# Decoder trunk on one core: block sums queued behind the inverse root, the low half of each hidden pair one pair later, and another order in the last stage

## Chip, core and metric

The kernel runs on one core of one Trainium2 chip. The metric is the device time of one execution in microseconds (us); lower is better. The engines are named as in the profile: PE (matrix products and transposes), PEld (its weight load), DVE (vector), ACT (scalar, activations), POOL (GpSimd) and SP (which issues most DMAs). Each engine works through its own instructions in order and waits on semaphores for the others. A small "q" behind an engine's name is its instruction queue, which issues DMAs.

## What is computed

Two decoder layers over 512 tokens of width 1024, in float32. The change touches the squared-ReLU MLP, which ends both layers, and the final RMS norm:

```python
def squared_relu_mlp(h, w1, w2):
    return jnp.square(jax.nn.relu(h @ w1)) @ w2
...
        x = x + squared_relu_mlp(rms_norm(x, norm_mlp[layer]), mlp_w1[layer], mlp_w2[layer])
...
    return rms_norm(x, final_norm)
```

with a hidden width of 4096, and rms_norm(x, g) = x / sqrt(mean(x^2) + eps) * g. Between the two MLPs stand the shared key/value projection and the attention of the second layer, which the change leaves alone.

## The kernel before

**Number format.** Each float32 matrix is split into a hi and a lo part in float16, and each product is three matmuls: hi x hi, hi x lo, lo x hi (lines 341 to 343 in the up stages, 550 to 552 in the down stages). The hi is written by ACT, the lo (value less hi) by DVE.

**Stages.** An MLP is up, down, up, down, with half of the hidden width each time (`first_half`, then `mlp_down` again).

- **Up stage** (`mlp_up`, lines 487 to 506): eight pairs of hidden chunks. A pair takes 48 matmuls of 512 columns into two PSUM banks out of six (a, b, c twice each). Then DVE takes the relu and scales it by the tokens' inverse root of the norm (line 499, tile `ml_t`, one buffer), ACT squares it (line 501, tile `ml_z`), POOL forms four block sums of the square (line 503), ACT writes the hi part `rh` (line 504) and DVE the lo part `rl` (line 505). In the first up stage of a layer the inverse root is computed while the first pair is on PE: PE sums the squares (`ss.rstd`), ACT takes the square root and DVE does five small operations (`rstd_of`, lines 295 to 306); PE spreads the result over the partitions (line 312) and ACT scales it into the tile `rb` (line 317).
- **Down stage** (`mlp_down`, lines 536 to 574): four passes, one for each pair of output chunks. A pass runs over eight chunks c and computes seven block products instead of eight (the form with sums and differences of 2x2 blocks by Strassen and Winograd): 21 matmuls of 256 columns for each c. The seven results lie in four banks, a a b b in even passes and c c d e in odd ones. `combine` (lines 508 to 534) adds the seven results of a finished pass into the residual X: one copy on ACT (`dn_p`, line 520) and nine operations on DVE. It is a generator whose parts are drawn one by one (`next(post)`) behind the c loop of the following pass.
- **Last down stage** (layer 1, second half): besides, `mid_b` transposes the chunks of X that are finished to token-major form (`token_major`): after c = 5 of a pass PE transposes into a bank (tag a or c), ACT takes a square with a sum for the final norm (line 1162) and a copy (line 1177), and POOL multiplies the copy by the gains (line 1178). The copies must be done before the next pass writes the same banks. In the last pass the eight chunks are cut: c 0 to 3 for all seven products, then each product by itself over c 4 to 7 in a written order (`last_b`), so that `stt` additions, transposes, squares, the inverse root of two token tiles, the scaling and the stores to `out` (`store`, lines 1188 to 1203) follow each other.

**Weights.** `pieces` lists all weight pieces in order. `load_piece` issues the DMAs on SP's queue, `convert_piece` turns a piece into hi (ACT) and lo (DVE): 128x1024 pieces for an up stage (tiles `wst`, `whi`, `wlo`; lines 195 and 196), and for a down stage blocks of two chunks, for which DVE first forms the four block sums `W_SUMS` (line 182) in the loaded tile, then hi (line 184) and lo (line 185, 128x1792). Three loaded blocks and four converted ones fit; a loaded block's buffer is free for the next DMA when its lo is written, a converted one's when PE has used it. `ahead()` converts up to two pieces, or three blocks, ahead of use; `drain(ahead())` is where this stands in the program.

**What sets the order.** Lines are traced in program order, but a scheduling pass of the framework puts each engine's instructions in the order in which they are expected to become ready. So the block sums of a down stage stand far ahead of their place in the program, between the instructions of the up stage. `tc.issue_after(ins)` puts those instructions of its block that run on the engine of `ins` behind `ins` in that order, without a semaphore.

Of the kernel before, what the change touches and what calls it, by code (L numbers as in the profile page):

```python
# [2 lines left out]

# [1 line left out]

# [43 lines left out]
def body(ctx, tc, x, rel_bias, norm_mix, norm_mlp, mlp_w1, mlp_w2, a_w_in, a_conv_w, a_w_out,  # L49
# [121 lines left out]
    def convert_piece(step=1024):  # L171

        i = pos["cv"]
        if i >= len(pieces):
            return
        _, shape, sc = pieces[i]
        t = staged.pop(i)
        pos["cv"] += 1
        if shape is None:
            b = t.rearrange("p (k b n) -> p k b n", k=2, n=128)  # L180
            for e, o, x, y in W_SUMS:
                DVE.tensor_tensor(b[:, :, o], b[:, :, x], b[:, :, y], op=e)  # L182
            hi, lo = (wk[0].tile([128, 2, 7, 128], F16, name=n, bufs=NW2) for n in ("whi2", "wlo2"))
            ACT.activation(hi, b[:, :, 1:], AF.Copy, scale=sc)  # L184
            DVE.scalar_tensor_tensor(lo, b[:, :, 1:], sc, hi, op0=OP.mult, op1=OP.subtract)  # L185
            ready[i] = (hi, lo)
            yield
        else:
            a, n = shape
            hi = wpool.tile([128, PIECE], F16, name="whi", bufs=NW)  # L190
            lo = wpool.tile([128, PIECE], F16, name="wlo", bufs=NW)
            for s in range(0, a * n, step):
                e = min(s + step, a * n)
                w = t[:, s:e]
                ACT.activation(hi[:, s:e], w, AF.Copy, scale=sc)  # L195
                DVE.scalar_tensor_tensor(lo[:, s:e], w, sc, hi[:, s:e], op0=OP.mult, op1=OP.subtract)  # L196
# [90 lines left out]
    def split_gain(dst, c, src, gname):  # L287
# [3 lines left out]
        DVE.scalar_tensor_tensor(dst[1][:, c], src, g, dst[0][:, c], op0=OP.mult, op1=OP.subtract)  # L291
        return hi

    def rstd_of(ss):
# [10 lines left out]
        DVE.scalar_tensor_tensor(r, t, 1.5, r, op0=OP.add, op1=OP.mult)  # L305
        return r

    def broadcast_rows(r):
# [177 lines left out]

    def mlp_up(xs, ss, rh, half, rb):
        turn[0] = 1
        for p in range(8):
            ph = [acc(), acc()]  # L490
            first = p == 0 and half == 0
            pair(xs, ph, mid=ss.rstd if first else None)
            if first:
                pr = broadcast_rows(ss.r)
                rb = row_tile(pr, math.sqrt(SR) / (SW * SX))
            drain(ahead())
            t = wk[0].tile([128, 2, S], F32, name="ml_t", bufs=1)
            for m in range(2):
                DVE.scalar_tensor_tensor(t[:, m], ph[m], 0.0, rb, op0=OP.max, op1=OP.mult)  # L499
            z = wk[0].tile([128, 8, 256], F32, name="ml_z", bufs=2)  # L500
            ACT.activation(z[:, 0:4].rearrange("p (m k) n -> p m (k n)", m=2), t, AF.Square)  # L501
            for e, o, a, b in R_SUMS:
                POOL.tensor_tensor(z[:, o], z[:, a], z[:, b], op=e)  # L503
            ACT.activation(rh[0][:, p], z[:, 1:8], AF.Copy)  # L504
            DVE.tensor_tensor(rh[1][:, p], z[:, 1:8], rh[0][:, p], op=OP.subtract)  # L505
        return rb

    def combine(p, acc7, done):

        sc = 1.0 / (SR * SW2)  # L510
        P1, P2, P6, P7, P5, P3, P4 = acc7
        X1, X2 = X[:, 2 * p + 1], X[:, 2 * p]
        n1, n2 = slice(256, 512), slice(0, 256)
        both = X[:, 2 * p:2 * p + 2, n2]

        def stt(o, ps, y):
            DVE.scalar_tensor_tensor(o, ps, sc, y, op0=OP.mult, op1=OP.add)

        p1 = wk[0].tile([128, 256], F32, name="dn_p", bufs=1)
        ACT.activation(p1, P1, AF.Copy, scale=sc)  # L520
# [10 lines left out]
        E.tensor_tensor(both, both, wv, op=OP.add)  # L531
        stt(X2[:, n1], P4, X2[:, n1])
        E.tensor_tensor(X2[:, n1], X2[:, n1], wv[:, 0], op=OP.add)
        yield
        if done:
            yield from done(p)

    def mlp_down(rh, done, mid=None, last=None):

        post = iter(())  # L540
        for p in range(4):
# [13 lines left out]
            for c in range(0, 4 if late else 8, 2):  # L555
                w = next_piece()
                for k in range(2):
                    for i in range(7):
                        product(i, c + k, [u[:, k] for u in w])
                    if c + k == 5 and mid:  # L560
                        mid(p)
                    if k == 0:
                        drain(ahead())
                    next(post, None)
            if late:
                drain(post)
                if mid:
# [3 lines left out]
                return  # L571
            drain(post)
            post = combine(p, acc7, done)
        drain(post)

    def first_half(hp, xs, ss):
# [568 lines left out]
    with pool("hidden_b") as hp:  # L1145
# [12 lines left out]
            return fng[p // 2][:, (p % 2) * 256:(p % 2) * 256 + n * 128]  # L1158

        def square(v, t, k):  # L1160
            junk = hp.tile([128, 2, S], F32, name="ml_t", bufs=1)[:, 0, 0:v.shape[1]]
            ACT.activation(junk, v, AF.Square, accum_out=ssf[:, t, k:k + 1])

        def turn_tokens(ps, t, tiles):
# [3 lines left out]
        def token_major(p, h, tag):  # L1168
# [4 lines left out]
            for i in range(2):  # L1173
                t = 2 * h + i
                v, o = ps[:, i * 256:(i + 1) * 256], xt[t][:, p * 256:(p + 1) * 256]
                square(v, t, p)
                ACT.activation(o, v, AF.Copy)
                POOL.tensor_tensor(o, o, gains(p), op=OP.mult)

        def mid_b(p):  # L1180
            if p:
                for h in range(2):
                    token_major(p - 1, h, "a" if p % 2 else "c")

        def done_b(p):
            yield

        def store(h, late=None):
            sst = work.tile([128, 2], F32, name="sst", bufs=2)
            DVE.tensor_reduce(sst, ssf[:, 2 * h:2 * h + 2], axis=mybir.AxisListType.X, op=OP.add)  # L1190
            r = rstd_of(sst)
            for i in range(2):
                t = 2 * h + i
                a, b = xt[t][:, 0:512], xt[t][:, 512:1024]
                ACT.activation(a, a, AF.Copy, scale=r[:, i:i + 1])
                if late:
                    b = xt[t][:, 512:768]
                    DVE.scalar_tensor_tensor(xt[t][:, 768:896], late[i], r[:, i:i + 1], gains(3, 1),
                                             op0=OP.mult, op1=OP.mult)
                    c = xt[t][:, 896:1024]  # L1200
                    DVE.tensor_scalar(c, c, r[:, i:i + 1], None, op0=OP.mult)
                DVE.tensor_scalar(b, b, r[:, i:i + 1], None, op0=OP.mult)
                nc.sync.dma_start(out[0, t * 128:(t + 1) * 128, :], xt[t])

        def last_b(acc7, product):

# [13 lines left out]
            product(2)  # L1220
            stt(wv[:, 1], P6, p1)
            DVE.tensor_tensor(X1[:, n1], X1[:, n1], p1, op=OP.add)
            product(3)
            stt(wv[:, 0], P7, wv[:, 1])
            DVE.tensor_tensor(both, both, wv, op=OP.add)
            product(4)
            stt(both, P5[:, None, :].to_broadcast([128, 2, 256]), both)
            product(5)
            stt(X1[:, n2], P3, X1[:, n2])
            DVE.tensor_tensor(X2[:, n1], X2[:, n1], wv[:, 0], op=OP.add)  # L1230
            product(1)
            stt(X1[:, n1], P2, X1[:, n1])
            for t in range(2):
                ps = bank("a")
                turn_tokens(ps, t, (6, 7))
                square(ps[:, 0:256], t, 3)
                DVE.tensor_tensor(xt[t][:, 768:1024], ps[:, 0:256], gains(3), op=OP.mult)
            store(0)
            for t in range(2, 4):
                ps = bank("b")  # L1240
                turn_tokens(ps, t, (7,))
                square(ps[:, 0:128], t, 3)
                DVE.tensor_tensor(xt[t][:, 896:1024], ps[:, 0:128], gains(3)[:, 128:256], op=OP.mult)
            product(6)
            stt(X2[:, n1], P4, X2[:, n1])
# [38 lines left out]
```

## Time and profile before

| | |
|---|---|
| Median of three runs | 1137.75 us (1135.86 to 1139.03) |
| The profiled execution's own time | 1136.88 us |
| Its span, first to last instruction | 1135.1 us |
| Granted PE clock, mean | 0.995 |
| Busy: PE, DVE, ACT, POOL | 1095.8, 832.3, 568.5, 157.6 us |
| HBM, mean | 99 GB/s |
| First MLP (up, down, up, down) | about 182 to 504 us of the span |
| Second MLP to the end | about 800 us to the end |

All times in the views count from the span's start. A row of a timeline has the start, the duration, the engine, the line of the kernel, the operation, out<-in by tile names, the shapes, and a count when several like it were merged; in brackets stands how long the engine sat idle before it, and what it waited for. A row of the list of waits says who waited for whom: us in total, how many times, the longest. Tiles have the names of the program without buffer numbers: `wst` and `wlo` stand for the up pieces and the down blocks alike, told apart by line and shape; `xsh` and `xsl` of lines 1177 and above are the token-major output tiles. Ends of matmuls are modelled: they start one behind the other, and a row's duration is longer than the distance to the next.

### The profile page before, as it was taken

What the parts mean: (1) busy time and instruction counts of PE and PEld (TensorE: products, weight loads), DVE (VectorE), ACT (ScalarE), POOL (GpSimd) and SP (SyncE); (2) the same over time, 40 slices, a digit from 0 to 9 for tenths busy, and PEclk for the clock granted to TensorE, in tenths of its full rate; (3) what the DMA queues carried; (4) which work ended last, traced back from release to release, by engine and by line L of the source; (5) the groups of instructions that cost most, each with busy time, mean ns of one, the idle gap of its engine ahead of it and who ended that gap; (6) DMA issues with size and microseconds to landing.
All of it is one profiled execution on the core that took longest, in us unless ns stands there. A gap on an engine that the chain in (4) does not pass through costs nothing.

```text
span 1135.1 us, 20099 instructions
## 1 busy us (share of the span) xinstructions
PE 1095.8 (97%) x7959; PEld 694.1 (61%) x7959; DVE 832.3 (73%) x1498; ACT 568.5 (50%) x922; POOL 157.6 (14%) x198
## 2 busy tenths in 40 slices
PE   8999999999999999999999989899999999999985
PEld 4444444446884448865767666664444787445874
DVE  4755458765897556999589969896895598754795
ACT  4532235444433444556679777765544433343452
POOL 0000000422000221001002022220122100123020
PEclk9999999999999999999999999999999999999998
DMA  6433335333333333313334341112633333330221
GB/s 210 130 94 97 107 105 172 113 93 113 112 112 112 111 95 107 112 42 120 112 78 122 83 138 38 39 38 74 187 111 112 111 109 115 105 95 7 84 84 75
DMA packets 149378, 115.75 MB, mean 102 GB/s; under 512 B 8612, under 2 KB 146564, under 8 KB 149284
## 3 DMA queue, kind: packets, MB, share of 16 engines
q1 hardware_dynamic: 146736, 109.47, 31.8%
q10 hardware_dynamic: 2260, 4.40, 1.3%
q8 instruction: 62, 1.02, 0.4%
q0 software_dynamic: 288, 0.61, 0.2%
q14 instruction: 32, 0.26, 0.1%
HBM read 110.22 MB, written 2.14 MB: 99 GB/s over the span
## 4 chain that ended last, share of the span: by engine, by line
PE 50%; DVE 19%; ACT 11%; issue 7%; POOL 7%; DMA 5%; SPq 1%; DVEq 0%; ACTq 0%; POOLq 0%
POOL ml_z L503 6%; PE a L341 4%; PE a L342 4%; PE a L343 4%; DVE wlo L185 4%; DMA wst<-mlp_w_dram 3%; ACT rh L504 3%; PE c L343 3%; PE c L342 3%; PE c L341 3%; PE b L342 3%; PE b L341 3%; PE b L343 3%; DVE wlo L196 3%; DVE ml_t L499 2%
## 5 line engine op out<-in xcount | busy, mean ns | idle before, releaser
L195 ACT ACTIVATE whi<-wst 128x1024 f16<-128x1024 f32 (+4 forms) x171 | 142.4, 858 | 127.9 <-PE b L342 38.4
L196 DVE SCALAR_TENSOR_TENSOR wlo<-wst,whi 128x1024 f16<-128x1024 f32 (+4 forms) x171 | 169.9, 1001 | 40.2 <-ACT whi L195 39.9
L503 POOL TENSOR_TENSOR ml_z<-ml_z 128x256 f32<-128x256 f32 x128 | 99.9, 801 | 610.1 <-ACT ml_z L501 410.1
L184 ACT ACTIVATE whi<-wst 128x1792 f16<-128x1792 f32 x64 | 106.9, 1692 | 135.4 <-DVE wst L182 102.3
L341 PEld LDWEIGHTS <-whi 128*128 128x128 f16 x1024 | 100.4, 98 | 112.3 <-issue 5.5
L343 PEld LDWEIGHTS <-wlo 128*128 128x128 f16 x1024 | 100.2, 98 | 112.1 <-issue 0.4
L342 PEld LDWEIGHTS <-whi 128*128 128x128 f16 x1024 | 100.2, 98 | 107.6 <-issue 2.0
L505 DVE TENSOR_TENSOR rl<-ml_z,rh 128x1792 f16<-128x1792 f32 x32 | 64.8, 2026 | 135.9 <-ACT rh L504 135.7
L185 DVE SCALAR_TENSOR_TENSOR wlo<-wst,whi 128x1792 f16<-128x1792 f32 x64 | 128.8, 2019 | 3.0 <-ACT whi L184 2.9
L182 DVE TENSOR_TENSOR wst<-wst 128x256 f32<-128x256 f32 x256 | 108.9, 469 | 24.4 <-DMA wst<-mlp_w_dram 23.4
L504 ACT ACTIVATE rh<-ml_z 128x1792 f16<-128x1792 f32 x32 | 54.3, 1698 | 106.1 <-POOL ml_z L503 106.1
L551 PEld LDWEIGHTS <-whi 128*128 128x128 f16 x896 | 87.7, 98 | 16.2 <-issue 5.6
L552 PEld LDWEIGHTS <-wlo 128*128 128x128 f16 x896 | 87.6, 98 | 15.0 <-issue 4.2
L550 PEld LDWEIGHTS <-whi 128*128 128x128 f16 x896 | 87.7, 98 | 10.5
L343 PE MATMUL b<-xsh,wlo 128*128 128x512 f16 x208 | 78.8, 379 | 0.0
L342 PE MATMUL b<-xsl,whi 128*128 128x512 f16 x208 | 78.8, 379 | 0.0
L341 PE MATMUL b<-xsh,whi 128*128 128x512 f16 x208 | 78.7, 379 | 0.0
L501 ACT ACTIVATE ml_z<-ml_t 128x1024 f32<-128x1024 f32 x32 | 33.8, 1057 | 88.4 <-DVE ml_t L499 88.4
L963 ACT ACTIVATE at_p<-at_s,at_m 128x128 f32<-128x128 f32 (+3 forms) x128 | 71.0, 557 | 13.7 <-DVE at_m L961 12.6
L551 PE MATMUL a<-rl,whi 128*128 128x256 f16 x256 | 69.8, 273 | 3.7 <-DVE rl L505 3.7
L341 PE MATMUL c<-xsh,whi 128*128 128x512 f16 x192 | 72.8, 379 | 0.0
L342 PE MATMUL c<-xsl,whi 128*128 128x512 f16 x192 | 72.8, 379 | 0.0
(309 smaller groups left out, 2686.4 us busy)
## 6 DMA issues: line engine op xcount, KB each, us to landing
wst<-mlp_w_dram SPq DMA_DIRECT2D x256, 256.0 KB, 3.3
wst<-a_w_in_dram SPq DMA_DIRECT2D x18, 512.0 KB, 3.5
wst<-w_kv_dram SPq DMA_DIRECT2D x12, 512.0 KB, 3.5
T<-ext_d ACTq DMA_DIRECT2D x4, 1056.0 KB, 6.0
wst<-a_w_out_dram SPq DMA_DIRECT2D x8, 512.0 KB, 3.4
wst<-b_w_qg_dram SPq DMA_DIRECT2D x8, 512.0 KB, 3.5
wst<-b_w_o_dram SPq DMA_DIRECT2D x8, 512.0 KB, 3.3
wst<-a_w_in_dram SPq DMA_DIRECT2D x8, 384.0 KB, 5.5
```

The lines of the kernel that those rows point to most:

```text
L182: DVE.tensor_tensor(b[:, :, o], b[:, :, x], b[:, :, y], op=e)
L184: ACT.activation(hi, b[:, :, 1:], AF.Copy, scale=sc)
L185: DVE.scalar_tensor_tensor(lo, b[:, :, 1:], sc, hi, op0=OP.mult, op1=OP.subtract)
L195: ACT.activation(hi[:, s:e], w, AF.Copy, scale=sc)
L196: DVE.scalar_tensor_tensor(lo[:, s:e], w, sc, hi[:, s:e], op0=OP.mult, op1=OP.subtract)
L341: PE.matmul(ps, w[0], xs[0], start=start, stop=False)
L342: PE.matmul(ps, w[0], xs[1], start=False, stop=False)
L343: PE.matmul(ps, w[1], xs[0], start=False, stop=stop)
L503: POOL.tensor_tensor(z[:, o], z[:, a], z[:, b], op=e)
L504: ACT.activation(rh[0][:, p], z[:, 1:8], AF.Copy)
L550: PE.matmul(acc7[i], wh, xh, start=c == 0 and not other, stop=False, skip_group_check=other)
L551: PE.matmul(acc7[i], wh, xl, start=False, stop=False, skip_group_check=other)
```

## The change

It has five parts.

1. The block sums of the down weights are put behind the last operation of the newest inverse root in DVE's order (`root_op`).
2. In the up stage the lo of a pair is traced after the relu of the next pair, and ordered behind it; `ml_t` gets a second buffer. The last pair's lo follows the loop.
3. In the down stage `combine` is advanced once as soon as its pass is over (copy and first two `dn_w` steps), and the next draws shift; the weight conversions at c = 0 are ordered behind that copy on ACT.
4. In the last down stage the conversions that stood after c = 4 come after c = 5, behind the last token-major copy on ACT.
5. In the tail, product 4 comes before product 3; the gain multiplication of the last token-major pieces is merged into their scaling (one operation with scale and gain in place of two), DVE scales all 768 other columns of tiles 0 and 1, for which ACT did 512; these stand behind the last addition to X (`final`); the stores of tiles 2 and 3 are cut into halves, the first on ACT's DMA queue, the second on SP's.

```diff
-            for e, o, x, y in W_SUMS:
-                DVE.tensor_tensor(b[:, :, o], b[:, :, x], b[:, :, y], op=e)
+            with tc.issue_after(root_op[0].ins):
+                for e, o, x, y in W_SUMS:
+                    DVE.tensor_tensor(b[:, :, o], b[:, :, x], b[:, :, y], op=e)
...
-        DVE.scalar_tensor_tensor(r, t, 1.5, r, op0=OP.add, op1=OP.mult)
+        root_op[0] = DVE.scalar_tensor_tensor(r, t, 1.5, r, op0=OP.add, op1=OP.mult)
...
-            t = wk[0].tile([128, 2, S], F32, name="ml_t", bufs=1)
+            t = wk[0].tile([128, 2, S], F32, name="ml_t", bufs=2)
             for m in range(2):
-                DVE.scalar_tensor_tensor(t[:, m], ph[m], 0.0, rb, op0=OP.max, op1=OP.mult)
+                relu = DVE.scalar_tensor_tensor(t[:, m], ph[m], 0.0, rb, op0=OP.max, op1=OP.mult)
+            if rest:
+                with tc.issue_after(relu.ins):
+                    rest()
...
-            DVE.tensor_tensor(rh[1][:, p], z[:, 1:8], rh[0][:, p], op=OP.subtract)
+            rest = lambda lo=rh[1][:, p], v=z[:, 1:8], hi=rh[0][:, p]: DVE.tensor_tensor(lo, v, hi, op=OP.subtract)
+        rest()
...
-        ACT.activation(p1, P1, AF.Copy, scale=sc)
+        copied[0] = ACT.activation(p1, P1, AF.Copy, scale=sc)
...
-                    if c + k == 5 and mid:
-                        mid(p)
-                    if k == 0:
-                        drain(ahead())
-                    next(post, None)
+                    behind = None
+                    if c + k == 0 and p:
+                        behind = copied[0]
+                    if c + k == 5 and mid and p:
+                        behind = mid(p)
+                    if k == (1 if c == 4 and mid else 0):
+                        with tc.issue_after(behind.ins) if behind else nullcontext():
+                            drain(ahead())
+                    if c + k or not p:
+                        next(post, None)
...
             post = combine(p, acc7, done)
+            next(post)
...
+            product(4)
+            stt(both, P5[:, None, :].to_broadcast([128, 2, 256]), both)
             product(3)
             stt(wv[:, 0], P7, wv[:, 1])
             DVE.tensor_tensor(both, both, wv, op=OP.add)
-            product(4)
-            stt(both, P5[:, None, :].to_broadcast([128, 2, 256]), both)
             product(5)
...
-                DVE.tensor_tensor(xt[t][:, 768:1024], ps[:, 0:256], gains(3), op=OP.mult)
-            store(0)
+                early.append(ps[:, 0:256])
+            r = root(0)
...
-                DVE.tensor_tensor(xt[t][:, 896:1024], ps[:, 0:128], gains(3)[:, 128:256], op=OP.mult)
+                early.append(ps[:, 0:128])
             product(6)
-            stt(X2[:, n1], P4, X2[:, n1])
+            final = DVE.scalar_tensor_tensor(X2[:, n1], P4, sc, X2[:, n1], op0=OP.mult, op1=OP.add)
...
-            store(1, late)
+            with tc.issue_after(final.ins):
+                for t in range(2):
+                    DVE.scalar_tensor_tensor(xt[t][:, 768:1024], early[t], r[:, t:t + 1], gains(3),
+                                             op0=OP.mult, op1=OP.mult)
+                    DVE.tensor_scalar(xt[t][:, 0:768], xt[t][:, 0:768], r[:, t:t + 1], None, op0=OP.mult)
+                    put(t, nc.sync)
+            r = root(1)
+            for i in range(2):
+                t, c = 2 + i, r[:, i:i + 1]
+                ACT.activation(xt[t][:, lo], xt[t][:, lo], AF.Copy, scale=c)
+                put(t, nc.scalar, lo)
+                DVE.scalar_tensor_tensor(xt[t][:, 768:896], late[i], c, gains(3, 1), op0=OP.mult, op1=OP.mult)
+                DVE.scalar_tensor_tensor(xt[t][:, 896:1024], early[t], c, gains(3)[:, 128:256],
+                                         op0=OP.mult, op1=OP.mult)
+                DVE.tensor_scalar(xt[t][:, 512:768], xt[t][:, 512:768], c, None, op0=OP.mult)
+                put(t, nc.sync, hi)
```

`root(h)` is the first two lines of the old `store` (sum of squares and inverse root of two token tiles), `put` one DMA to `out`, `lo` and `hi` the columns 0 to 511 and 512 to 1023. In `token_major`, the last copy on ACT is returned so that the conversions can be ordered behind it.

More of the change, by code (lines that the diff above doesn't have):

```diff
@@ L1 @@
 import math
-from contextlib import ExitStack
+from contextlib import nullcontext, ExitStack
 import numpy as np
@@ L292, in split_gain @@
         return hi
+    root_op = [None]
     def rstd_of(ss):
@@ L488, in mlp_up @@
         turn[0] = 1
+        rest = None
         for p in range(8):
@@ L504, in mlp_up @@
             ACT.activation(rh[0][:, p], z[:, 1:8], AF.Copy)
-            DVE.tensor_tensor(rh[1][:, p], z[:, 1:8], rh[0][:, p], op=OP.subtract)
+            rest = lambda lo=rh[1][:, p], v=z[:, 1:8], hi=rh[0][:, p]: DVE.tensor_tensor(lo, v, hi, op=OP.subtract)
+        rest()
         return rb
+    copied = [None]
     def combine(p, acc7, done):
@@ L1160, in square @@
         def square(v, t, k):
-            junk = hp.tile([128, 2, S], F32, name="ml_t", bufs=1)[:, 0, 0:v.shape[1]]
+            junk = hp.tile([128, 2, S], F32, name="ml_t", bufs=2)[:, 0, 0:v.shape[1]]
             ACT.activation(junk, v, AF.Square, accum_out=ssf[:, t, k:k + 1])
@@ L1176, in token_major, with root, put @@
                 square(v, t, p)
-                ACT.activation(o, v, AF.Copy)
+                last = ACT.activation(o, v, AF.Copy)
                 POOL.tensor_tensor(o, o, gains(p), op=OP.mult)
+            return last
         def mid_b(p):
-            if p:
-                for h in range(2):
-                    token_major(p - 1, h, "a" if p % 2 else "c")
+            return [token_major(p - 1, h, "a" if p % 2 else "c") for h in range(2)][1]
         def done_b(p):
             yield
-        def store(h, late=None):
+        def root(h):
             sst = work.tile([128, 2], F32, name="sst", bufs=2)
             DVE.tensor_reduce(sst, ssf[:, 2 * h:2 * h + 2], axis=mybir.AxisListType.X, op=OP.add)
[L1191 to L1203, printed above, removed]
+            return rstd_of(sst)
+        def put(t, queue, at=slice(0, D)):
+            queue.dma_start(out[0, t * 128:(t + 1) * 128, at], xt[t][:, at])
         def last_b(acc7, product):
@@ L1232, in last_b @@
             stt(X1[:, n1], P2, X1[:, n1])
+            lo, hi = slice(0, 512), slice(512, 1024)
+            early = []
             for t in range(2):
```

## Prediction

> **What bounds the kernel now.** I read first the busy times by windows over the two MLPs, then the list of who waited for whom on PE, then the timelines around each wait. The windows of ten microseconds have columns for PE, its weight load, DVE, ACT, POOL, clock, DMA share and GB/s; the two sums are those from 180 to 540 us and from 770 us to the end.
>
> ```profile
> span 1135.1 us, 20099 instructions
> 230.00:240.00 10.00, 10.00 (x48) 4.51 (x47) 5.74 (x6) 4.46 (x5) 2.82 (x4) 1.00 0.37 107
> 300.00:310.00 10.00, 10.00 (x94) 8.95 (x93) 9.51 (x17) 5.00 (x5) 0.00 (x0) 1.00 0.39 119
> sum 360.00, PE 356.67 PEld 231.06 DVE 274.82 ACT 170.08 POOL 56.62; mean PE 9.91 PEld 6.42 DVE 7.63 ACT 4.72 POOL 1.57
> sum 370.00, PE 345.62 PEld 223.74 DVE 259.59 ACT 156.97 POOL 61.08; mean PE 9.34 PEld 6.05 DVE 7.02 ACT 4.24 POOL 1.65
> ```
>
> PE is the bound. In an up stage (230 to 240) DVE has over 4 us of 10 free; in a down stage (300 to 310) only 0.5. No edit removes a matmul, so all that can be won is PE's idle time where the diff reaches: 3.3 us in the first MLP, 19.4 us in the second up to the end of the span (365.1 us from 770, less 345.6), of which the last 9 are the end after PE's last instruction. The list of waits names what ended PE's gaps (total us, times, longest):
>
> ```profile
> PE a L551 <- DVE rl L505: 3.7, 3, 1.8
> PE a L550 <- ACT xsh L1177: 2.5, 1, 2.5
> PE e L312 <- DVE rs_r L305: 1.8, 2, 0.9
> PE c L1166 <- DVE X L1213: 1.5, 1, 1.5
> PE c L550 <- DVE dn_w L1213: 0.8, 1, 0.8
> PE a L1166 <- DVE X L531: 0.6, 1, 0.6
> PE a L550 <- ACT xsl L1177: 0.5, 1, 0.5
> PE c L550 <- ACT xsl L1177: 0.5, 1, 0.5
> PE c L550 <- ACT xsh L1177: 0.4, 1, 0.4
> ```
>
> Together 12.3 us. I call the four up/down pairs A1, A2 (layer 0) and B1, B2 (layer 1).
>
> **1. Block sums behind the inverse root.** DVE at A1, and the sums at B1:
>
> ```profile
> 190.00 0.76 DVE L182 TENSOR_TENSOR wst<-wst 128x256 f32<-128x256 f32 x2 [1.32 <-DMA wst<-mlp_w_dram]
> 190.83 1.99 DVE L185 SCALAR_TENSOR_TENSOR wlo<-wst,whi 128x1792 f16<-128x1792 f32 x1
> 193.56 0.15 DVE L305 SCALAR_TENSOR_TENSOR rs_r<-rs_t,rs_r 128x4 f32<-128x4 f32 x1
> 806.89 1.10 DVE L182 TENSOR_TENSOR wst<-wst 128x256 f32<-128x256 f32 x3 [2.19 <-DMA wst<-mlp_w_dram]
> ```
>
> The root's five small operations stand behind sums that wait for a block's transfer (1.32 and 2.19 us idle) and around a 2 us lo. In the new order they stand in one run ahead of all sums: at A1 they start when PE has given its sums of squares and ACT the root, and end near 190, over 3 us earlier, while PE asks for the result 0.9 us before it came. Both gaps close: 1.8 us (bounds 0 and 1.8; I take 1.8, the slack is three times the gap). What is late next: the sums, the first block's lo and, since SP's queue is in order, the block transfers that wait for that lo's buffer, with up-stage weights behind them. I work the lo's out as 2 to 5 us later than before; that is the fourth rival.
>
> **2. The lo one pair later.** At the end of A1 (`rl` is the lo, `ml_t` the relu, `rh` the hi):
>
> ```profile
> 266.19 0.38 PE L343 MATMUL c<-xsh,wlo 128*128 128x512 f16 x1
> 271.91 1.99 ACT L195 ACTIVATE whi<-wst 128x1024 f16<-128x1024 f32 x2
> 272.03 2.03 DVE L505 TENSOR_TENSOR rl<-ml_z,rh 128x1792 f16<-128x1792 f32 x1 [4.70 <-ACT rh L504]
> 273.98 1.22 DVE L196 SCALAR_TENSOR_TENSOR wlo<-wst,whi 128x1024 f16<-128x1024 f32 x1
> 275.11 1.28 DVE L499 SCALAR_TENSOR_TENSOR ml_t<-c,rb 128x512 f32<-128x512 f32 x2
> 276.43 1.06 ACT L501 ACTIVATE ml_z<-ml_t 128x1024 f32<-128x1024 f32 x1 [2.53 <-DVE ml_t L499]
> 280.50 1.70 ACT L504 ACTIVATE rh<-ml_z 128x1792 f16<-128x1792 f32 x1 [3.01 <-POOL ml_z L503]
> 282.23 2.03 DVE L505 TENSOR_TENSOR rl<-ml_z,rh 128x1792 f16<-128x1792 f32 x1 [4.70 <-ACT rh L504]
> 284.31 0.27 PE L551 MATMUL a<-rl,whi 128*128 128x256 f16 x1 [1.58 <-DVE rl L505]
> ```
>
> PE ends the last pair at 266.4; its relu starts at 275.1, though DVE sat idle 4.70 us just before. It is queued behind the lo of the pair before, and that waits for relu, square, POOL's sums and hi of its own pair: a ring. From relu to relu it takes relu 1.2, square 1.1, POOL 3.0, hi 1.7, lo 1.95, weight lo 1.15: 10.1, hardly less than the 10.3 that PE takes for a pair (48 matmuls, as in the window 230 to 240). So the 9 us of lag from the stage's start are never made up. In the new order the relu goes ahead of that lo. A ring remains, since two weight lo's stand between, and the second waits for a weight hi that ACT does after its hi: 1.2 + 1.1 + 3.0 + 1.7 + 1.0 (half of the 1.99) + 1.15 = 9.15. It gains 1.2 us a pair, and the lag starts at 2 to 3 us instead of 7 to 10; by the last pair it is gone. The last lo is then written at 266.4 + 1.3 + 1.1 + 3.0 + 1.7 + 2.0, about 275.6, and PE wants it at 282.7: all three gaps close, 3.7 us (bounds 0, if the ring stays, and 3.7; I take 3.7, 7 us of slack). The second `ml_t` buffer only allows this. A2 and B2 get the same lead.
>
> **3. Last down stage, B2: weights behind the token copies.** In the rows, b8 to b15 are the last eight of its 16 weight blocks. The L1177 copies free the banks that the next pass writes:
>
> ```profile
> 1040.48 0.38 PE L343 MATMUL c<-xsh,wlo 128*128 128x512 f16 x1
> 1047.32 1.28 DVE L499 SCALAR_TENSOR_TENSOR ml_t<-c,rb 128x512 f32<-128x512 f32 x2
> 1073.75 2.02 DVE L185 SCALAR_TENSOR_TENSOR wlo<-wst,whi 128x1792 f16<-128x1792 f32 x1
> 1075.79 0.88 SPq L157 DMA_DIRECT2D wst<-mlp_w_dram  x2
> 1076.26 3.29 ACT L184 ACTIVATE whi<-wst 128x1792 f16<-128x1792 f32 x2 [3.18 <-DVE wst L182]
> 1077.99 2.02 DVE L185 SCALAR_TENSOR_TENSOR wlo<-wst,whi 128x1792 f16<-128x1792 f32 x1 [0.42 <-ACT whi L184]
> 1080.87 0.27 PE L550 MATMUL a<-rh,whi 128*128 128x256 f16 x1 [2.46 <-ACT xsh L1177]
> 1081.43 2.71 DVE L182 TENSOR_TENSOR wst<-wst 128x256 f32<-128x256 f32 x4 [1.41 <-DMA wst<-mlp_w_dram]
> ```
>
> ACT sat idle 3.18 us with the copies next but two, behind the hi's of b9 and b10 (1076.26). Now the copies go first: their transposes are done near 1074, 2.5 us of ACT work end near 1076.3, two microseconds before PE's next pass at 1078.4, and b9's hi starts when it did before. PE loses none of 2.5 + 0.5 at the third pass and 0.5 + 0.4 at the fourth: 3.9 us.
>
> The price is on DVE. In the new order the lo of b9 (1077.99) stands behind the sums of b11, whose transfer is issued only when the lo of b8 has freed its buffer (1075.79, right at the end of 1073.75). With the old times: issue 1075.8, sums begin 1081.4, 2.7 us, lo 2.0: 1086.1, while PE, no longer held, wants b9 one block (42 matmuls, 4.6 us by the pace of the window 300 to 310) after 1078.4, at 1083.0: a stall of 3 us. The same stands at b13, a pass later. What speaks against it is part 2: in B2 the last relu was 6.6 us late (1040.7 to 1047.3), so the lo's of b4 and b5, and every transfer behind them, start some 6 us earlier; I get b11's transfer issued near 1068 and b9's lo at 1080, bound by its hi. At b13 I get 1099 to 1100 against a need at 1102.4. I take 3.9 (bounds 3.9 and, with 3 to 4 us of stall at both places, minus 4).
>
> Those 2.71 us for four sums against 0.76 for two are DVE beside POOL's multiplications. The Trainium skill ("SBUF — State Buffer", section on the two separate sides) calls the port pair of the two engines an exclusive lock, so that one operation waits out the other; by it the sums of b14 and b15, which now meet the multiplications, would take 2.7 instead of 1.4 each. The trace agrees in size; b13's slack covers one such delay, not two.
>
> "Finished pairs summed at once" only puts the first three operations of a pass's combine earlier in the program; in A and B1 the new order on ACT and DVE is the old one there: 0. The order edges themselves carry no semaphore: 0.
>
> **4. The tail.**
>
> ```profile
> 1115.07 0.44 ACT L1219 ACTIVATE dn_p<-c 128x256 f32<-128x256 f32 x1
> 1125.00 0.41 DVE L1213 SCALAR_TENSOR_TENSOR X<-e,X 128x256 f32<-128x256 f32 x1
> 1127.76 0.16 DVE L1190 TENSOR_REDUCE sst<-ssf 128x2 f32<-128x10 f32 x1 [0.91 <-ACT ml_t L1162]
> 1130.25 0.35 DVE L1202 TENSOR_SCALAR xsl<-xsl,rs_r 128x256 f32<-128x256 f32 x1
> out_dram<-xsl SPq DMA_DIRECT2D x2, 512.0 KB, 3.0
> ```
>
> Product 4 goes ahead of product 3, which waits for `dn_p` (1115.07) and the P6 step after it: a whole product of 1.3 us instead of 0.6 us of it covers the wait, and the 0.8 gap falls to about 0.2. The X of L531, 0.6 late, was queued behind the last block's lo; earlier weights bring it to about PE's time: 0.5. The four multiplications of lines 1237 and 1243 go, and ACT no longer scales two 512-wide tiles between its last two squares, so the last sum of squares waits for DVE alone. Counting from the transposes before product 0, I get the last X addition (1125.00) 1.1 us and the last `sst` (1127.76) 1.5 us earlier. DVE does more ahead of it, two 768-wide scalings that no row shows: by the 256-wide one (0.35) between 0.35 and 1.05 each; I take 0.6. From `sst` to the last scaling the 2.8 us stay. Tail: 0.5 + 1.5 = 2.0 (bounds 0.6 and 3).
>
> The stores of the last two token tiles are halved, one half on ACT's queue. The Trainium skill ("DMA: Bandwidth & Descriptors", section on issuing engines) says that queues of several engines share the same 16 DMA engines and save issue time alone; by it the 3.0 us of landing hardly shrink. I take 0 for this, and up to 0.7 stands in the 3 above.
>
> **Sum**: 1.8 + 3.7 + 3.9 + 2.0 = 11.4 us off the profiled execution's 1136.88 (span 1135.1): 1125.5. The median of the three runs is 0.9 higher, which would give 1126.3; I forecast **1126.0**.
>
> **Rivals.**
> - **The weight lo's of B2 come late.** PE's bank waits turn into waits for `wlo` at b9 and b13. For: b11's transfer waited for above took 5.6 us from issue to sums, and POOL's port. Against: the 6 us lead. Part 3 becomes between 0 and minus 4: 1130 to 1134.
> - **The ring stays** (the change doesn't do what it says in the up stages): if the second weight lo comes behind yet another hi, relu still lags at the end and the 3.7 us stay, and with them most of the B2 lead: 1130.
> - **Nothing moves**, PE's gaps going elsewhere one for one, as DVE at 9.5 of 10 in the down stages could make them: 1136 to 1138.
> - **Slower: SP's queue.** The third block's hi now stands behind pair 0's hi on ACT, so its lo is some 5 us later, near 206, the next block transfer waits for it, and the up-stage weights behind that one wait too. PE wants those weights two or three pairs of 10.3 us on, about 235 (three pairs before 266.4); allowing 10 us for transfer, hi and lo, each microsecond of that lo after 225 costs PE one, in A1 and in B1. To end over 0.3% above before it would have to be at 232 (7.4 us twice against 11.4 saved and 3.4 added). 206 is far from it.
>
> **How the numbers follow.** Forecast as summed, 1123.5 to 1128: 0.62. Late weight lo's: 0.17. Ring stays: 0.10. Nothing moves: 0.05. Slower: 0.03. The rest, 0.03, is a larger gain in the tail. The range 1122.5 to 1131.5 takes in the tail's bounds, the ring, and B2 up to about 1.5 us of stall, and leaves out some 0.17. A measurement of this kernel tells about 0.3% (3.4 us) from no change: faster 0.88 (the first three cases but for the worst of the second, and the rest), same 0.08, slower 0.04.
>
> **What would show it.** PE's waits for `rs_r` and `rl` gone, each relu within 1 to 2 us of PE's last matmul of its pair from the fifth pair on; PE's waits for the L1177 copies (now 1193) gone with no wait for `wlo` at the third and fourth pass of B2; the last `sst` some 11.2 us after `dn_p` instead of 12.7 (1127.76 less 1115.07). It is wrong if PE waits for `wlo` in B2, if relu still starts 8 us late in A1's last pair, or if weights are missing on PE within A1 or B1.

## Result and profile after

| | before | after |
|---|---|---|
| Median | 1137.75 us | 1149.86 us (1148.95 to 1152.49) |
| Ratio to before | | 1.0113, interval 1.0096 to 1.013 |
| Profiled execution | 1136.88 us, span 1135.1 | 1149.57 us, span 1147.8 |
| POOL busy | 157.6 us | 206.8 us |

The change made the kernel 12 us slower; forecast were 12 us faster. Where the time went is read best by stages. The boundaries below are the starts of the first matmul of each stage, so a row is one stage: A1 up, A1 down, A2 up, A2 down, B1 up, B1 down, B2 up (left out: all of it PE's busy time, in both), and B2 down with the end. Columns: length; busy PE, PEld, DVE, ACT, POOL; granted clock; DMA share; GB/s. First after, then before.

```profile
180.67:269.25 88.58, 85.02 (x397) 38.51 (x396) 57.68 (x74) 40.12 (x37) 33.08 (x24) 1.00 0.41 119
269.25:351.26 82.01, 76.49 (x673) 66.91 (x672) 66.87 (x100) 31.97 (x25) 8.83 (x8) 0.96 0.34 104
351.26:434.14 82.88, 82.88 (x387) 37.59 (x384) 51.70 (x61) 34.20 (x30) 24.90 (x24) 1.00 0.35 105
434.14:512.03 77.89, 75.34 (x673) 66.60 (x672) 66.07 (x100) 34.69 (x36) 8.75 (x8) 0.98 0.29 86
810.81:895.30 84.49, 84.30 (x397) 38.82 (x396) 62.41 (x76) 41.26 (x38) 31.77 (x24) 1.00 0.46 137
895.30:976.62 81.32, 75.90 (x673) 66.59 (x672) 64.57 (x96) 31.81 (x24) 8.84 (x8) 0.96 0.35 104
...
1059.63:1147.77 88.14, 77.80 (x705) 69.02 (x703) 63.54 (x111) 36.72 (x71) 16.93 (x20) 0.97 0.24 78
```

```profile
181.11:266.41 85.30, 84.40 (x398) 38.86 (x397) 61.70 (x78) 40.91 (x38) 22.41 (x24) 1.00 0.42 124
266.41:341.51 75.10, 73.52 (x674) 65.74 (x673) 60.55 (x93) 31.16 (x23) 5.64 (x8) 1.00 0.37 113
341.51:424.39 82.88, 82.88 (x387) 37.55 (x385) 52.39 (x65) 34.64 (x30) 17.29 (x25) 1.00 0.36 108
424.39:498.71 74.32, 73.87 (x674) 65.55 (x672) 61.61 (x96) 34.39 (x35) 5.25 (x8) 1.00 0.28 87
797.22:882.48 85.26, 84.34 (x397) 38.87 (x396) 65.01 (x80) 41.94 (x38) 21.12 (x24) 1.00 0.47 136
882.48:957.82 75.34, 73.55 (x674) 65.75 (x673) 60.00 (x93) 31.33 (x23) 5.64 (x8) 1.00 0.38 113
...
1040.69:1135.10 94.41, 78.58 (x705) 69.00 (x703) 65.09 (x112) 38.61 (x73) 14.88 (x20) 0.96 0.22 73
```

Row by row, after less before: A1 up +3.3, A1 down +6.9, A2 up 0, A2 down +3.6, B1 up -0.8, B1 down +6.0, B2 up +0.1, B2 down and the end -6.3; together +12.8. So the last stage gained about what the prediction gave it (3.9 and 2.0), and the first three down stages lost 16.5 us. Of those, 9.7 are PE standing (length less PE's busy time: 5.5, 2.6 and 5.4, before 1.6, 0.5 and 1.8), and 6.8 are PE being busy longer with the same matmuls, at a clock of 0.96 to 0.98. The other column that moved is POOL: 24.90 instead of 17.29 us in A2's up stage, for no more sums.

What PE waited for in the changed kernel (total us, times, longest):

```profile
PE a L560 <- ACT rh L511: 7.0, 3, 3.1
PE a L561 <- DVE rl L512: 6.5, 5, 1.8
PE a L344 <- ACT whi L196: 2.4, 1, 2.4
PE a L1182 <- DVE X L541: 0.7, 1, 0.7
PE c L1182 <- DVE X L1253: 0.7, 1, 0.7
```

The waits for `rs_r` and for the token copies are gone, as forecast. The waits for the hidden pair's lo (3.7 us) have not gone but grown to 13.5 us: now the hi `rh` is late too. The timeline of one pair in A1, a 128x1792 `rl` on DVE beside POOL's four sums, then the stage's end:

```profile
260.37 2.01 DVE L512 TENSOR_TENSOR rl<-ml_z,rh 128x1792 f16<-128x1792 f32 x1
261.62 1.35 POOL L510 TENSOR_TENSOR ml_z<-ml_z 128x256 f32<-128x256 f32 x1 [6.30 <-ACT ml_z L508]
262.31 1.75 DVE L197 SCALAR_TENSOR_TENSOR wlo<-wst,whi 128x1024 f16<-128x1024 f32 x1
262.94 1.70 POOL L510 TENSOR_TENSOR ml_z<-ml_z 128x256 f32<-128x256 f32 x1
264.61 0.72 POOL L510 TENSOR_TENSOR ml_z<-ml_z 128x256 f32<-128x256 f32 x1
265.40 0.72 POOL L510 TENSOR_TENSOR ml_z<-ml_z 128x256 f32<-128x256 f32 x1
266.16 1.70 ACT L511 ACTIVATE rh<-ml_z 128x1792 f16<-128x1792 f32 x1 [4.61 <-POOL ml_z L510]
267.76 1.99 ACT L196 ACTIVATE whi<-wst 128x1024 f16<-128x1024 f32 x2
268.83 1.22 DVE L197 SCALAR_TENSOR_TENSOR wlo<-wst,whi 128x1024 f16<-128x1024 f32 x1 [4.78 <-ACT whi L196]
271.17 2.01 DVE L512 TENSOR_TENSOR rl<-ml_z,rh 128x1792 f16<-128x1792 f32 x1
287.75 1.70 ACT L511 ACTIVATE rh<-ml_z 128x1792 f16<-128x1792 f32 x1 [4.61 <-POOL ml_z L510]
289.50 0.27 PE L560 MATMUL a<-rh,whi 128*128 128x256 f16 x1 [3.12 <-ACT rh L511]
291.56 0.37 PE L561 MATMUL a<-rl,whi 128*128 128x256 f16 x1 [1.79 <-DVE rl L512]
```

POOL's third and fourth sum take 0.72 us. The first takes 1.35: it begins at 261.62 and ends 0.6 after `rl` has (262.38). The weight lo, begun at 262.31, takes 1.75 instead of 1.22. POOL's second sum takes 1.70 and ends 0.6 after that weight lo (264.06). The two engines take turns, and the one that comes second stands until the first has finished. The four sums end at 266.12, 4.5 us after their start, where they took 2.9 before. Everything behind is in the ring: the hi, the weight hi, the weight lo that waits for it, the next relu. From `rl` to `rl` it is 10.80 us (260.37 to 271.17), PE's pair 10.3: the lag grows instead of shrinking. The last `rh` comes at 287.75 and PE stands for it.

Behind the first of these two waits PE's clock halves, and it stays low for some 7 us. Two windows of one microsecond (the one ahead of the first has a clock of 0.94, the one behind the last 1.00):

```profile
290.00:291.00 1.00, 0.00 (x0) 0.00 (x0) 1.00 (x1) 1.00 (x2) 0.00 (x0) 0.50 0.00 0
296.00:297.00 1.00, 1.00 (x7) 0.77 (x6) 0.00 (x0) 0.00 (x0) 0.00 (x0) 0.64 0.74 258
```

### The profile page after: what moved, and what is told of

Its sections match the earlier page's. It is cut to its first block, busy times and chain, and to the rows that moved or that the text cites. A ratio compares the mean times of both kernels' runs of the same rounds, so it can differ in the third digit from the quotient of the medians.

```text
span 1147.8 us, 20109 instructions
## 1 busy us (share of the span) xinstructions
PE 1105.5 (96%) x7959; PEld 699.8 (61%) x7959; DVE 840.4 (73%) x1496; ACT 566.0 (49%) x920; POOL 206.8 (18%) x198
## 4 chain that ended last, share of the span: by engine, by line
PE 69%; DVE 9%; POOL 7%; ACT 6%; issue 6%; DMA 3%; SPq 0%; DVEq 0%; ACTq 0%; POOLq 0%
POOL ml_z L510 6%; PE a L344 5%; PE a L345 5%; PE a L346 5%; PE b L346 4%; PE b L345 4%; PE b L344 4%; PE c L344 4%; PE c L345 4%; PE c L346 4%; PE c L985 2%; PE c L560 2%; PE c L561 2%; PE c L562 2%; ACT whi L196 2%
## 5 line engine op out<-in xcount | busy, mean ns | idle before, releaser
L197 DVE SCALAR_TENSOR_TENSOR wlo<-wst,whi 128x1024 f16<-128x1024 f32 (+4 forms) x171 | 183.3, 1078 | 152.9 <-ACT whi L196 152.6
L510 POOL TENSOR_TENSOR ml_z<-ml_z 128x256 f32<-128x256 f32 x128 | 148.5, 1179 | 577.0 <-ACT ml_z L508 380.5
L183 DVE TENSOR_TENSOR wst<-wst 128x256 f32<-128x256 f32 x256 | 100.9, 439 | 26.8 <-DMA wst<-mlp_w_dram 25.7
L560 PE MATMUL a<-rh,whi 128*128 128x256 f16 x256 | 71.0, 277 | 7.0 <-ACT rh L511 7.0
L346 PE MATMUL c<-xsh,wlo 128*128 128x512 f16 x192 | 72.8, 379 | 0.5 <-DVE wlo L197 0.5
```

The lines of the kernel that those rows point to most:

```text
L346: PE.matmul(ps, w[1], xs[0], start=False, stop=stop)
L560: PE.matmul(acc7[i], wh, xh, start=c == 0 and not other, stop=False, skip_group_check=other)
```

## Experiments

Two theories stood at the start. **P**: DVE's lo and weight lo, now beside POOL's sums, hold POOL up; the ring becomes longer than PE's pair; all loss is part 2's. **W**: the loss begins with the block sums behind the root (part 1), which make the first stage's weights late. Ratios are to the kernel before on the same chip, with their intervals; its median there was 1139.57 us for the first four runs, 1137.08 for the next four and 1138.8 for the last two.

**1. root_only.** Before, with part 1.

```diff
-            for e, o, x, y in W_SUMS:
-                DVE.tensor_tensor(b[:, :, o], b[:, :, x], b[:, :, y], op=e)
+            with tc.issue_after(root_op[0].ins):
+                for e, o, x, y in W_SUMS:
+                    DVE.tensor_tensor(b[:, :, o], b[:, :, x], b[:, :, y], op=e)
```

> The kernel before with part 1 alone (block sums behind the inverse root). Theory P (POOL's sums, slowed by the lo and the weight lo on DVE, close a ring of 10.8 us a pair, and all loss comes from part 2): PE's two waits for the inverse root go, 1.8 us, and nothing else moves, 1135 to 1137. Theory W (the loss begins with the sums that were moved behind the root, which make the first stage's weights late): PE waits 2 to 3 us for a weight hi in the third pair of a layer's first up stage, 1138 to 1142.

1136.88 us, ratio 0.9979 (0.9969 to 0.9988), 1.4 to 3.5 us faster. No wait for `rs_r`, none for a weight hi. W falls; the 1.8 us of the prediction lie in the interval.

**2. lo_only.** Before, with part 2.

```diff
-            t = wk[0].tile([128, 2, S], F32, name="ml_t", bufs=1)
+            t = wk[0].tile([128, 2, S], F32, name="ml_t", bufs=2)
...
+            if rest:
+                with tc.issue_after(relu.ins):
+                    rest()
...
-            DVE.tensor_tensor(rh[1][:, p], z[:, 1:8], rh[0][:, p], op=OP.subtract)
+            rest = lambda lo=rh[1][:, p], v=z[:, 1:8], hi=rh[0][:, p]: DVE.tensor_tensor(lo, v, hi, op=OP.subtract)
```

> The kernel before with part 2 alone (the lo of a pair after the next pair's relu, two ml_t buffers). Theory P: from relu to relu 10.8 us, POOL's four sums 4.5 us instead of 2.9, and PE's waits for rh and rl at the start of the down stages, with the slower clock behind them, cost what they cost in the changed kernel: 6.9, 3.6 and 6.0 us in A1, A2 and B1, so 1151 to 1157. Theory W: the ring is shorter than PE's pair, the waits for rl go, 1133 to 1136.

1154.79 us, ratio 1.0139 (1.0123 to 1.0155). POOL's sums take 4.5 us from the fourth pair on, the ring 10.80. Part 2 alone costs 14 to 18 us; the whole change cost 11 to 15.

**3. no_lo.** The changed kernel without part 2 (that diff taken back).

> The changed kernel without part 2 (each lo at its own pair again, one ml_t buffer). Theory P: the root's 1.8 us and the 6.3 us of the last down stage stay, the rest is as before: 1128 to 1131; if the weight lo's of B2 come late without the earlier relu of part 2, up to 1134. Theory W: the loss stays, 1144 or more.

1135.83 us, ratio 0.9963 (0.995 to 0.9975): the loss is gone, and P's second case holds (1134 by a before of 1137.75; here before stood at 1139.57). PE's waits of no_lo from 1042 us, B2's down stage:

```profile
PE a L1177 <- DVE X L536: 2.8, 2, 2.5
PE a L557 <- DVE wlo L186: 1.8, 1, 1.8
```

Parts 3 and 4 did take the copy waits away (3.9 us), but a late weight lo in the third pass (1.8) and an addition to X in the fourth, which stands on DVE behind three weight lo's, cost as much instead (2.8, of which 0.6 were there before). This is the prediction's first rival, in the kernel without the earlier relu.

**4. lo_gate.** The changed kernel; before each deferred lo, DVE copies one column of POOL's last sum of the newer pair.

```diff
-            if rest:
-                with tc.issue_after(relu.ins):
-                    rest()
             z = wk[0].tile([128, 8, 256], F32, name="ml_z", bufs=2)
             ACT.activation(z[:, 0:4].rearrange("p (m k) n -> p m (k n)", m=2), t, AF.Square)
             for e, o, a, b in R_SUMS:
                 POOL.tensor_tensor(z[:, o], z[:, a], z[:, b], op=e)
+            if rest:
+                g = wk[0].tile([128, 1], F32, name="ml_g", bufs=2)
+                with tc.issue_after(relu.ins):
+                    mark = DVE.tensor_copy(g, z[:, 7, 0:1])
+                with tc.issue_after(mark.ins):
+                    rest()
```

> The changed kernel with one more operation on DVE ahead of each deferred lo: a copy of one column of POOL's last sum of the newer pair, so that the lo waits until POOL has finished and the two no longer meet. Theory P: POOL's four sums are back at 2.9 to 3.1 us, the ring is 9.2 us a pair, relu catches up with PE, the waits at the start of the down stages go, 1124 to 1129, although DVE has more work and one more wait. Theory W, or any theory by which the later lo or its place is itself the loss: 1148 or more.

1122.26 us, ratio 0.9854 (0.9838 to 0.9871). The timeline of lo_gate in A1:

```profile
252.41 1.28 DVE L503 SCALAR_TENSOR_TENSOR ml_t<-a,rb 128x512 f32<-128x512 f32 x2
254.86 2.90 POOL L507 TENSOR_TENSOR ml_z<-ml_z 128x256 f32<-128x256 f32 x4 [6.31 <-ACT ml_z L505]
257.79 0.15 DVE L511 COPY ml_g<-ml_z 128x1 f32<-128x1 f32 x1 [2.97 <-POOL ml_z L507]
257.86 2.02 DVE L515 TENSOR_TENSOR rl<-ml_z,rh 128x1792 f16<-128x1792 f32 x1
261.60 1.28 DVE L503 SCALAR_TENSOR_TENSOR ml_t<-b,rb 128x512 f32<-128x512 f32 x2
```

DVE stands 2.97 us on purpose, POOL is back at 2.90, and from relu to relu it is 9.19 us, where the prediction had worked out 9.15. PE has no gap in the first three down stages (73.36 us each, all busy). One more operation and one more wait make the changed kernel some 28 us faster (1149.86 to 1122.26; by the two ratios, 29).

**5 and 6. gate_sbuf and gate_psum.** lo_gate, with 2 us of work on DVE while POOL sums. They differ in where DVE's inputs lie, and in the operation: one of 128x1792, or three of 128x512.

In both, the copy and the forming of the mark in lo_gate's diff become:

```diff
+                with tc.issue_after(relu.ins):
+                    mark = DVE.tensor_copy(g, z[:, 0, 0:1])
+                with tc.issue_after(mark.ins):
+                    ...
+                with tc.issue_after(mark.ins):
                     mark = DVE.tensor_copy(g, z[:, 7, 0:1])
```

In gate_sbuf the middle is the lo itself, once more than needed (`zs` lists the `z` tiles):

```diff
+                    mark = DVE.tensor_tensor(rh[1][:, p - 1], zs[-2][:, 1:8], rh[0][:, p - 1], op=OP.subtract)
```

In gate_psum it is:

```diff
+                    for _ in range(3):
+                        mark = DVE.scalar_tensor_tensor(rh[1][:, p - 1, 0:2].rearrange("p k n -> p (k n)"), ph[1], 0.0, rb,
+                                                        op0=OP.max, op1=OP.mult)
```

> The kernel of run lo_gate, in which DVE now does something while POOL sums: after a copy of one column of the square (so that it starts when POOL does) it forms the deferred lo once more than needed, 2.0 us with two inputs in SBUF. The result is the same. Theory P (POOL stands while DVE reads two inputs from SBUF): POOL's four sums 4.3 to 4.9 us instead of 2.9, from relu to relu 10.6 to 11.2 us, the waits at the start of the down stages are back, 1134 to 1156. Theory Q (the ring is set by DVE's order alone, POOL's length is a by-product): the extra 2.0 us lie in DVE's idle time, the ring stays at 9.2 and the time at 1122 to 1124.

> The control to gate_sbuf: the same place and about the same 2.0 us on DVE, but three operations that read one input from PSUM (the pair's accumulator) and one from SBUF, and write where the lo goes, which is then overwritten. Theory P in its narrow form (only DVE operations with two inputs in SBUF hold POOL up): POOL 2.9 to 3.0 us, ring 9.2 to 9.4, 1121 to 1125. In its wide form (any DVE work beside POOL holds it up): POOL 4.3 to 4.9, ring 10.6 or more, as gate_sbuf.

gate_sbuf: 1161.49 us, ratio 1.0214 (1.0196 to 1.0232). gate_psum: 1123.25 us, ratio 0.9876 (0.9859 to 0.9893). Timelines in A1, gate_sbuf first:

```profile
252.36 4.68 POOL L509 TENSOR_TENSOR ml_z<-ml_z 128x256 f32<-128x256 f32 x4 [6.64 <-ACT ml_z L507]
252.38 2.58 DVE L515 TENSOR_TENSOR rl<-ml_z,rh 128x1792 f16<-128x1792 f32 x1
263.37 2.58 DVE L515 TENSOR_TENSOR rl<-ml_z,rh 128x1792 f16<-128x1792 f32 x1
```

```profile
253.61 1.28 DVE L503 SCALAR_TENSOR_TENSOR ml_t<-a,rb 128x512 f32<-128x512 f32 x2
256.05 2.91 POOL L507 TENSOR_TENSOR ml_z<-ml_z 128x256 f32<-128x256 f32 x4 [6.30 <-ACT ml_z L505]
256.08 2.13 DVE L514 SCALAR_TENSOR_TENSOR rl<-a,rb 128x512 f16<-128x512 f32 x3
262.81 1.28 DVE L503 SCALAR_TENSOR_TENSOR ml_t<-b,rb 128x512 f32<-128x512 f32 x2
```

With two inputs in SBUF DVE holds POOL up (4.68) and is held up itself (2.58 instead of 2.0): the ring is 10.99 us and all is lost. With one input in PSUM the two run side by side: POOL 2.91, ring 9.20. P holds in its narrow form, and Q falls: in gate_sbuf DVE itself stands 2.11 us for POOL behind the extra work. That it is the inputs and not the kind or the length of the operation, other rows show: in the changed kernel the weight lo, a `scalar_tensor_tensor` like gate_psum's but with two inputs in SBUF, held POOL up (1.70), and in before short block sums and POOL's multiplications met at 1081.43 (2.71 us for four sums, where two take 0.76 alone). The Trainium skill ("SBUF — State Buffer", section on who interferes with whom) says just this: a DVE instruction with two SBUF inputs contends with a GpSimd instruction that reads SBUF, the second to come stands until the first is done, and one with at most one SBUF input does not contend (outside certain modes); the rows agree. The price of gate_sbuf, 22 to 26 us, is above the 18 at most expected (1156 less 1137.75); the mechanism's two sizes (POOL, ring) are inside what was expected. By stages, gate_sbuf's profile is longer than before's by 7.6, 4.6 and 6.7 us in the first three down stages, 18.9 together, and the loss there is all that the expectation counted. It left out the up stages (5.6, 2.1 and 1.7 us longer in A1, B1 and B2, where PE waits for weight hi's and lo's) and the last stage, where PE waits 3.5 us for `rl` and of the changed kernel's gain of 6.3 us only 0.6 is left.

**7. gate_only.** Before, with part 2 and lo_gate's copy, none of the other parts.

> The kernel before with part 2 and the wait for POOL alone (no sums behind the root, no token copies ahead, old tail). Expected, from the stages of lo_gate against before: A1, A2 and B1 down give 1.7, 0.8 and 2.0 us, the last down stage at most 2 more, since its weights come earlier; 4 to 7 us below before. If parts 1 and 3 to 5 were worth nothing it would reach 1122 to 1124, as lo_gate.

1127.09 us, ratio 0.991 (0.9896 to 0.9924): 9 to 12 us faster, more than expected. The three down stages gave 4.7 us (73.36 each against 75.10, 74.32 and 75.34), and B2's down stage, where at most 2 were expected, 5.5. There PE waits for no token copy, without parts 3 and 4; its two waits left are the tail's (X 1.2 us, `dn_w` 0.8).

**8. tail_only.** Before, with part 5 (the whole tail of the diff).

> The kernel before with part 5 alone (product 4 before product 3, gains merged, halved stores). By the prediction's term 1.5 to 2.0 us below before (its wait for the last block's X stays, 0.6), and the last sum of squares about 11.2 us after dn_p instead of 12.7. If the merged scalings or the two queues cost what they save: 0 to plus 1.

1135.57 us, ratio 0.9986 (0.9977 to 0.9995): 0.6 to 2.6 us faster, as expected. From `dn_p` to the last `sst` it is 10.6 us.

**9. copies_only.** Before, with parts 3 and 4.

> The kernel before with parts 3 and 4 alone (finished pairs summed at once, conversions of the last down stage behind the token copies). By the prediction's term 3.9 us below before. By its first rival (without an earlier relu the weight lo's of b9 and b13 come late), as no_lo suggests: PE's waits for the copies go, a wait of about 1.8 us for wlo and one of about 2.5 for X come in their place, within 1 us of before.

1137.66 us, ratio 0.9997 (0.9987 to 1.0007): nothing. PE's waits from 1041 us to the end:

```profile
PE a L1174 <- DVE X L533: 2.5, 1, 2.5
PE a L554 <- DVE wlo L185: 1.2, 1, 1.2
```

The copy waits became waits for a weight lo and for X. PE waits 1.4 us more for X in the tail, as before (1.5).

**10. gate_no34.** lo_gate with parts 3 and 4 taken back.

> The kernel of run lo_gate without parts 3 and 4 (so the kernel before with parts 1, 5 and the gated part 2). If the token copies ahead of the conversions are worth their 3.9 us once the weights have their lead, this is 3 to 4 us slower than lo_gate, 0.3% or more, with PE waiting for xsh and xsl copies. If the earlier relu alone takes those waits away, as gate_only suggests, it is within 1 us of lo_gate and PE waits for no copy.

1122.4 us, ratio 0.986 (0.9839 to 0.9881), like lo_gate within the measurement, and PE waits for no copy. The last stage, where parts 3 and 4 act, is 87.23 us long, in lo_gate 87.25. So with lo_gate's early relu, parts 3 and 4 are worth nothing.

## Why the prediction was wrong

**The step that failed** is the ring of the second part: "1.2 + 1.1 + 3.0 + 1.7 + 1.0 (half of the 1.99) + 1.15 = 9.15. It gains 1.2 us a pair". The 3.0 for POOL is a row of before, and where it was read, at the end of A1, DVE does nothing while POOL sums: its weight lo is done just ahead of them (276.31 to 277.53, POOL from 277.56), and then it stands 4.70 us for the hi. That idle time was where the new order put the lo and a weight lo. I took the duration over and changed the company. With 4.5 in place of 3.0 the sum is 10.65, measured 10.80, against PE's 10.3; the sign of the step turns. The rest of the sum was right, as lo_gate shows: POOL kept clear, the ring is 9.19. I had the rule in hand, cited it further on for the block sums of B2, and priced there a possible 1.3 us; nothing in the prediction asked it of the ring. The trace of before had the size as well. POOL's sums of A1's first and fourth pair:

```profile
201.19 5.64 POOL L503 TENSOR_TENSOR ml_z<-ml_z 128x256 f32<-128x256 f32 x4 [197.56 <-DMA wst<-mlp_w_dram]
236.80 2.90 POOL L503 TENSOR_TENSOR ml_z<-ml_z 128x256 f32<-128x256 f32 x4 [7.29 <-ACT ml_z L501]
```

In the first three pairs, while weight lo's and block sums run on DVE, the same four sums take 5.64, 5.08 and 3.47 us; only from the fourth on is it 2.90. The row repeats, and I had taken one of its durations.

Of the cases given, "the ring stays" came nearest; none had a ring that becomes longer.

**Root: right.** Both `rs_r` waits are gone; 1.8 forecast, 1.4 to 3.5 measured alone. In the changed kernel A1 does not show it, since PE waits 2.37 us for a weight hi at the start of the sixth pair (POOL's row is that of the third):

```profile
227.21 6.51 POOL L510 TENSOR_TENSOR ml_z<-ml_z 128x256 f32<-128x256 f32 x4 [8.31 <-ACT ml_z L508]
236.46 0.39 PE L344 MATMUL a<-xsh,whi 128*128 128x512 f16 x1 [2.37 <-ACT whi L196]
```

That is close to the place of the fourth rival (weights missing near 235), but not its mechanism: the weight hi is queued on ACT behind a hi that waits for POOL, whose sums take 6.51 us beside the lo, the weight lo and six block sums. Neither part 1 alone nor part 2 alone shows such a wait in A1: it takes the moved block sums and the deferred lo together, so these 2.4 us are not part 2's by itself.

**Lead and token copies: right sum, wrong cause.** In the changed kernel the waits for copies are gone and none for `wlo` came in B2, so 3.9 is there. But copies_only gains nothing and gate_no34 loses nothing. In lo_only, which has part 2 without parts 3 and 4, 0.9 of the 3.9 us are left (0.43 and 0.46 at the third pass). So most of the gain is the early relu's: with it the block conversions are done before the copies come up on ACT. In gate_no34 the last copy ahead of the third pass ends at 1069.45 and PE begins that pass at 1070.52, without a wait; in before the copy ended at 1082.1, and PE was ready at 1078.4. The changed kernel has that lead in B2 alone: in the last pairs of that stage, with no more up weights to convert, it is 4.8 and 5.9 us from relu to relu (1049.55, 1054.35, 1060.21), so that the last relu is within half a microsecond of PE's end of the stage (1059.8). The prediction had said that the lead decides about the rival of the late weight lo's; no_lo and copies_only show that rival without the lead.

**Tail: right in its sum, in part by luck.** The rows of the changed kernel:

```profile
1129.68 0.44 ACT L1225 ACTIVATE dn_p<-c 128x256 f32<-128x256 f32 x1
1138.83 0.61 DVE L1264 TENSOR_SCALAR xsh<-xsh,rs_r 128x768 f32<-128x768 f32 x1
1140.28 0.15 DVE L1205 TENSOR_REDUCE sst<-ssf 128x2 f32<-128x10 f32 x1
1142.89 0.34 DVE L1274 TENSOR_SCALAR xsl<-xsl,rs_r 128x256 f32<-128x256 f32 x1
```

From `dn_p` to the last `sst` it is 10.6 us (11.2 forecast, 12.7 before), 2.1 us gained where 1.5 were forecast. The other term, 0.5 for the X of the last finished block, did not come: PE still waits 0.7 us for it (line 541 in the list of waits above; 0.6 before). In lo_gate, where the weights have their lead, that wait is gone. Besides, the 768-wide scaling takes 0.61 us (0.6 taken), and from `sst` to the last scaling it is 2.6 instead of 2.5. The halved stores on two queues bring nothing: the last one lands 6.3 us after that `sst` (1146.56), before 6.2. Forecast was 0.

**What was not in the sum at all**: the slower clock behind a wait, 6.8 of the 16.5 us lost. Two figures of the prediction are off by a tenth, and nothing hangs on them: 365.1 less 345.6 is 19.5, and the last lo's sum comes to 275.5.

What stays open: why in gate_sbuf the up weights come late, and what parts 3 and 4 are worth in the changed kernel itself, since no run takes them alone out of it. The best kernel here is lo_gate, 1122.26 us, with gate_no34 equal to it and simpler.

## What to carry to other kernels

A duration from a profile holds for the neighbours that the instruction had there: when a change fills an engine's idle time, ask which other engine worked in that time and what the two share. When work goes round several engines, add up the ring with the slowed durations and compare it with the bound engine's period; here 9.2 us against 10.3 made a lag vanish, and 10.8 made it grow. And an engine that waits on purpose (here 3 us of 9) can be worth more than one that is kept busy.

## What was unexpected of the hardware

**The clock drops after shorter waits than I would have thought.** In root_only a single wait of 2.10 us was followed by about 3 us at half clock; in before, 2.46 us at the same place were not (the row at 1080.87 above, clock 1.00 in the windows behind). Row and window of root_only:

```profile
1080.26 0.27 PE L553 MATMUL a<-rh,whi 128*128 128x256 f16 x1 [2.10 <-ACT xsh L1180]
```

```profile
1081.00:1082.00 1.00, 0.78 (x5) 0.39 (x4) 1.00 (x2) 0.87 (x5) 1.00 (x2) 0.50 0.78 232
```

The Trainium skill ("TensorE: Matmul & The Clock Gate", section on what is actually happening) describes a gate that halves the clock after an idle window of about 3.4 us that runs free of the program. The half clock agrees, and that equal waits end differently suits a window that runs free; that 2.10 us can be enough does not follow from it. By these rows a wait of 2.1 us with 3 us at half clock behind it costs about 3.6 us (2.1 and half of 3).
